# Issuing a decoder layer's transposed units from ScalarE's queue instead of SP's

## The chip, the core and the metric

The kernel runs on one core of a Trainium2 chip. The core has five engines that run side by side, each with its own instruction queue: TensorE (PE in the profile), VectorE (DVE), ScalarE (ACT), GpSimd (POOL) and SyncE (SP). SP computes nothing; it issues DMA transfers. ScalarE and GpSimd can issue transfers too, in between their own work. An instruction that waits holds back those behind it on its engine. The metric is the device time of one execution in microseconds (us).

## What is computed

One hybrid decoder layer on a sequence of 512 tokens of width 2048: a normalisation, one input projection whose columns feed three groups of heads, one output projection, a residual sum and a last normalisation.

```python
h = rmsnorm(x, norm_g)
proj = h @ w_in                      # 2048 x 8224, split into 19 parts
# A: 8 heads: compressed blocks, selected blocks, sliding window 512, mixed by gates
q_a = heads(a_q, A_HEADS)
o_a = gate[..., 0:1] * o_cmp + gate[..., 1:2] * o_slc + gate[..., 2:3] * o_win
y_a = o_a.reshape(bsz, T, A_WIDTH) * jax.nn.silu(a_z)
# B: mLSTM, 4 heads of 256, causal convolution before it, norm and two gates behind it
y_b = h_b.reshape(bsz, T, B_WIDTH) * jax.nn.silu(b_z)
# C: 8 heads, sliding window 128, with sinks
y_c = o_c.reshape(bsz, T, C_WIDTH) * jax.nn.silu(c_z)
mix = jnp.concatenate([y_a, y_b, y_c], axis=-1)
return x + mix @ w_out               # then rmsnorm with final_norm_g
```

## The kernel before

**The weight stream.** The two projections run through the whole kernel and set its order. The weights come in column groups (`groups`, then `outs`), each group in pieces of two (for `ck` four) row blocks of 128. A piece is loaded by SP (`dma_piece`, L140, 512 KB), split into a high and a low half by ScalarE (`wh`, L164 and L162) and VectorE (`wl`, L172 and L170), and multiplied on TensorE in three products for each row block (`mms`, L1149). While piece `pos` is multiplied, piece `pos + 2` is split and piece `pos + 5` is loaded at its end; there are three `raw` tiles.

**Steps and lanes.** A piece is multiplied in four parts, and behind each part, which is six matmuls, `step()` runs. It takes one turn of each generator in `lanes`: the heads' work is written as such generators, and `yield` ends a turn. So everything else is woven into the weight stream by hand, a step at a time, and the number of `yield`s between two pieces of work is the time that the first one has. The instructions then run in this order on each engine.

**The transposed units.** The softmax weights of A and C have queries on the partitions, and the product with the values needs keys there. `flip` turns them: for each part VectorE transposes blocks of 32 by 32 into `sq` (L613), the block is written to DRAM (`far`, L615) and read back in another order (`ptT` for A, `cptT` for C, L621). `a_out` flips eight units, one for each pair of heads and each of two branches, in six parts (widths 512, 512 and 256 for each of two heads); `c_out` flips four, in four parts (384 and 512 for each head). Behind the flip, `pause(PT_)` or `pause(PTC)` lets some steps pass, and then TensorE multiplies (`oT`, L952, and `coT`, L1035). Before the change SP issues all these transfers, in program order between the loads of weights.

**The same for B.** `hb_post` flips B's heads out in eight parts of 512 (tile `hb`), long before they are needed; `ev_bz` reads four of them back at once (`hbT`) behind the first part of groups `bz0` and `bz1`.

**What feeds the units.** `a_scores` works one unit ahead: scores on TensorE, a masked minimum on VectorE (L905), exponentials on ScalarE (L907), and scalings of the parts on ScalarE (L919) once VectorE has the sums' reciprocals (`wgt`, L913 and L914). It starts a unit only when the one before the last has been multiplied (`done`). `c_scores` does the same for C (L995, L998, L1004, L1012).

Of the kernel before, what the change touches and what calls it, by code (L numbers as in the profile page):

```python
# [27 lines left out]
T, D, P = 512, 2048, 128  # L28
# [32 lines left out]
def hymba_layer(ctx, tc, x, norm_g, w_in, w_out, pe_k, w1_k, w2_k, pe_v, w1_v, w2_v, conv_w, conv_b,  # L61
                i_bias, f_bias, mnorm_g, sinks, final_g, consts, out):
    nc = tc.nc
    PE, ACT, DVE, POOL, SP = nc.tensor, nc.scalar, nc.vector, nc.gpsimd, nc.sync
# [9 lines left out]
    def U(name, dt=F32):  # L74
        return ar.tile([P, 516], dt, tag="u", name=name)
# [3 lines left out]
    def WK(name):  # L79
        return ps.tile([P, 512], F32, tag="wk", bufs=4, name=name)  # L80
# [223 lines left out]
    p = WK("gT")  # L304
# [303 lines left out]
    def flip_out(src, tag, bufs):  # L608


        n = src.shape[1]
        sq, far = U("sq"), dr.tile([P * 512], F32, name="far", tag=tag, bufs=bufs)
        DVE.transpose(sq[:, :n].rearrange("p (j b t) -> p b j t", j=4, t=32),  # L613
                      src.rearrange("p (b k j) -> p b j k", j=4, k=32))
        SP.dma_start(far[:P * n].rearrange("(p f) -> p f", p=P), sq[:, :n])  # L615
        return far, n

    def flip_in(far, name):

        dst, (src, n) = U(name), far  # L620
        SP.dma_start(dst[:, :n].rearrange("p (q f) -> p q f", q=4),  # L621
                     src[:P * n].rearrange("(q p f) -> p q f", q=4, p=P))
        return dst[:, :n].rearrange("p (q b t) -> p b q t", q=4, t=32)

    def hb_post(pair, ssq):
        yield from pause(3)
        for t in range(4):
            hb, th = B["hb", pair, t], U("bsq")
            for q in range(2):
                ACT.activation(th[:, q * 256:(q + 1) * 256], hb[:, q * 256:(q + 1) * 256], AF.Square,  # L630
                               accum_out=ssq[:, 2 * t + q:2 * t + q + 1])
            yield
        r = S("br", 8, 2)
        rsqrt(r, ssq, 256, "b")
        DVE.tensor_scalar(r, r, 0.5, None, op0=OP.mult)
        yield
        for t in range(4):
            hb = B["hb", pair, t]
            for q in range(2):
                s = slice(q * 256, (q + 1) * 256)  # L640
                DVE.tensor_scalar(hb[:, s], hb[:, s], r[:, 2 * t + q:2 * t + q + 1], None, op0=OP.mult)
            yield

        B["hbT", pair] = []
        for t in range(4):
            B["hbT", pair].append(flip_out(B.pop(("hb", pair, t))[:, :512], "hbT", 8))
            yield
# [3 lines left out]
    def ev_bz(pair):  # L651
        def ev(c, acc):
            z = U("zf")
            scaled(z[:, :512], acc)
            if c == 0:
                B["hbT", pair] = [flip_in(x, "hbT") for x in B["hbT", pair]]
            start(bz_post(pair, c, z))
        return ev
# [198 lines left out]


    PB = {0: (1, 384), 1: (2, 0), 2: (1, 0), 3: (0, 0)}
    PT_, PTC = 6, 8  # L860
    ready = {}

    def flip(parts, name):

        far, back = [], []
        for i in range(len(parts)):
            far.append(flip_out(parts[i], "far", 8))
            parts[i] = None
            if i >= 2:
                back.append(flip_in(far[i - 2], name))  # L870
            yield
        return back + [flip_in(x, name) for x in far[-2:]]

    def a_scores():
        while B["cmp"] in lanes:
# [48 lines left out]
    def a_out():  # L924
        n = 0
        for pr in range(4):
# [3 lines left out]
            for br, vo in ((1, 0), (2, 128)):  # L930
                while n not in ready:
                    yield
                pt = ready.pop(n)
                yield from pause(PA)
                bl = ((3, 3, 3, 3), (2, 2, 2, 0), (1, 1))
                parts = [pt[h].pop(0)[:, :P * len(b)] for h in hs for b in bl]
                del pt
                back = yield from flip(parts, "ptT")
                tt = {h: {(j, b % (j + 1)): back[3 * q + u][:, b] for u in range(3) for b, j in enumerate(bl[u])}
                      for q, h in enumerate(hs)}  # L940
                yield from pause(PT_)

                if br == 1:
                    ob = WK("oT")
                    for q in range(2):
                        o = (pr % 2) * 128 + 64 * q
                        PE.matmul(ob[64 * q:64 * q + 64], vbd[g][:, o:o + 64], PCT[g][:, :512],
                                  start=True, stop=False, skip_group_check=True)
                for i in range(4):
                    for j in range(i, 4):  # L950
                        for q, h in enumerate(hs):
                            PE.matmul(ob[64 * q:64 * q + 64, j * P:(j + 1) * P], VG[i][:, vo + 64 * g:vo + 64 * g + 64],  # L952
                                      tt[h][j, i], start=False, stop=(br == 2 and i == 3), skip_group_check=True)
                done[n] = True
                n += 1
                yield
# [59 lines left out]
    def c_out():  # L1016

        blocks = [(0, 0), (1, 0), (1, 1), (2, 1), (2, 2), (3, 2), (3, 3)]
        for pr in range(4):
            while pr not in cready:  # L1020
                yield
            hs = (2 * pr, 2 * pr + 1)
            g = pr // 2
            pt = cready.pop(pr)
            yield from pause(PC)
            parts = [pt[h].pop(0)[:, 128 - 128 * u:512] for h in hs for u in range(2)]
            del pt
            back = yield from flip(parts, "cptT")
            tt = {h: {ji: back[2 * q + u][:, b] for u in range(2) for b, ji in enumerate(blocks[3 * u:3 + 4 * u])}
                  for q, h in enumerate(hs)}  # L1030
            yield from pause(PTC)
            ob = WK("coT")
            for n, (j, i) in enumerate(blocks):
                for q, h in enumerate(hs):
                    PE.matmul(ob[64 * q:64 * q + 64, j * P:(j + 1) * P], VG[i][:, 280 + 64 * g:344 + 64 * g],  # L1035
                              tt[h][j, i], start=(i < j or j == 0), stop=(i == j),
                              skip_group_check=True)
            cdone[pr] = True
            yield
            y_out("c", pr, ob)  # L1040
# [116 lines left out]
    for pos, (g, i) in enumerate(pieces):  # L1157
        np_ = KT // g.kps
        nct = g.n // P if g.mode == "F" else NT
        if i == 0:  # L1160
# [10 lines left out]
            if g.mode == "O":  # L1171
                n = int(g.name[3])
# [65 lines left out]
```

## Time and profile before

| | |
|---|---|
| three timed runs | 1027.75, 1028.22 and 1030.64 us, median 1028.22 |
| profiled execution, its own time | 1031.22 us |
| span from first to last instruction | 1029.5 us |
| granted TensorE clock, mean over the span | 0.989 of full speed |
| busy: PE, DVE, ACT, POOL | 1007.5, 585.6, 477.5, 21.5 us |
| writes `far<-sq` (L615) | 72, at 532.3 to 855.6 us |
| reads of `ptT`, `cptT`, `hbT` (L621) | 48, 16 and 8, at 536.8 to 860.9 us |

The profile is of one execution. A row with SPq or ACTq is a transfer's issue on that engine's queue; the transfer itself lands later. The page names a wait by what released it. The granted clock is what the chip allowed TensorE: 1.00 is 2.4 GHz, and the lower of its two levels is 1.2 GHz.

### The profile page before, as it was taken

The numbers are of one execution on the slowest core, as the hardware profiler recorded it, in microseconds if no ns is written. First come the engines' busy times: TensorE is split into PE (matmuls) and PEld (weight loads), VectorE is DVE, ScalarE is ACT, GpSimd is POOL, SyncE is SP. The second block draws the span as 40 slices with busy tenths as digits, with TensorE's granted clock in tenths as the row PEclk, the third lists the DMA queues.
The fourth block names the chain that finished last, engine by engine and source line by source line (L and its number), as shares of the span: only waits on it lengthen the run. The fifth ranks groups of instructions, "written<-read, shape, count | busy, mean of one in ns | idle before, by whom it ended". The sixth has DMA issues, their size and how long they took to land.

```text
span 1029.5 us, 13708 instructions
## 1 busy us (share of the span) xinstructions
PE 1007.5 (98%) x4967; PEld 835.0 (81%) x4967; DVE 585.6 (57%) x1253; ACT 477.5 (46%) x991; POOL 21.5 (2%) x40
## 2 busy tenths in 40 slices
PE   9999999999999999999999999999899899999996
PEld 7988888888888888888888788878777788888885
DVE  4563266664284847435566577856676575424434
ACT  6753244443253536234467474755654542323324
POOL 2400000000000000000000000000000000000000
PEclk9999999999999999999999999999999899999998
DMA  8633323232313244232335556555564685433214
GB/s 238 173 109 100 103 65 103 62 103 82 103 61 103 62 127 100 82 111 74 103 105 175 175 172 193 148 160 163 164 200 133 241 276 173 127 100 100 85 61 164
DMA packets 121092, 133.22 MB, mean 129 GB/s; under 512 B 23557, under 2 KB 81261, under 8 KB 120897
## 3 DMA queue, kind: packets, MB, share of 16 engines
q1 hardware_dynamic: 117792, 125.66, 40.9%
q0 software_dynamic: 2240, 6.23, 1.8%
q8 instruction: 39, 0.64, 0.3%
q10 hardware_dynamic: 992, 0.46, 0.2%
q14 instruction: 29, 0.23, 0.1%
HBM read 111.88 MB, written 20.45 MB: 129 GB/s over the span
## 4 chain that ended last, share of the span: by engine, by line
PE 86%; DVE 6%; DMA 5%; issue 1%; ACT 1%; SPq 0%; ACTq 0%; DVEq 0%
PE acc L1149 72%; DMA far<-sq 3%; DVE sq L613 2%; PE oT L952 2%; PE sp L561 1%; DMA ptT<-far 1%; PE acc L316 1%; PE acc L315 1%; PE acc L314 1%; DVE wl L172 1%; PE coT L1035 1%; PE sc L902 1%; PE sc L901 1%; PE xT L285 1%; DVE pp L905 0%
## 5 line engine op out<-in xcount | busy, mean ns | idle before, releaser
L1149 PE MATMUL acc<-hTh,wh 128*128 128x512 f32 x720 | 283.6, 394 | 0.0
L1149 PE MATMUL acc<-hTh,wl 128*128 128x512 f32 x720 | 281.5, 391 | 0.0
L1149 PE MATMUL acc<-hTl,wh 128*128 128x512 f32 x720 | 281.2, 391 | 0.0
L172 DVE SCALAR_TENSOR_TENSOR wl<-raw,gcol,wh 128x512 fp32r<-128x512 f32 (+1 forms) x256 | 179.0, 718 | 125.1 <-ACT wh L164 124.7
L164 ACT ACTIVATE wh<-raw,gcol 128x512 fp32r<-128x512 f32 (+1 forms) x256 | 171.2, 695 | 150.9 <-PE acc L1149 124.2
L1149 PEld LDWEIGHTS acc<-hTh,wl 128*128 128x128 f32 x720 | 135.4, 188 | 28.8
L1149 PEld LDWEIGHTS acc<-hTh,wh 128*128 128x128 f32 x720 | 135.6, 188 | 27.7 <-issue 1.7
L1149 PEld LDWEIGHTS acc<-hTl,wh 128*128 128x128 f32 x720 | 135.7, 188 | 25.8
L1149 PE MATMUL acc<-wh,hTh 128*128 128x512 f32 x256 | 101.2, 395 | 0.0
L1149 PE MATMUL acc<-wh,hTl 128*128 128x512 f32 x256 | 100.1, 391 | 0.0
L1149 PE MATMUL acc<-wl,hTh 128*128 128x512 f32 x256 | 99.9, 390 | 0.0
L1149 PE MATMUL acc<-wh,mixh 128*128 128x512 f32 x224 | 88.6, 396 | 0.0
L1149 PE MATMUL acc<-wh,mixl 128*128 128x512 f32 x224 | 88.1, 393 | 0.0
L1149 PE MATMUL acc<-wl,mixh 128*128 128x512 f32 x224 | 88.0, 393 | 0.0
L170 DVE TENSOR_TENSOR wl<-raw,wh 128x512 fp32r<-128x512 f32 x56 | 38.4, 689 | 55.7 <-ACT wh L162 55.4
L162 ACT CAST wh<-raw 128x512 fp32r<-128x512 f32 x56 | 34.0, 617 | 76.3 <-PE acc L1149 64.0
L1149 PEld LDWEIGHTS acc<-wh,hTl 128*128 128x128 f32 x256 | 48.0, 188 | 10.5
L1149 PEld LDWEIGHTS acc<-wh,hTh 128*128 128x128 f32 x256 | 48.1, 188 | 9.4 <-issue 0.4
L1149 PEld LDWEIGHTS acc<-wl,hTh 128*128 128x128 f32 x256 | 48.1, 188 | 9.0
L907 ACT ACTIVATE pp<-pp,nmx 128x512 f32<-128x512 f32 (+3 forms) x64 | 35.8, 559 | 35.1 <-DVE nmx L905 35.0
L905 DVE CUSTOM_DVE_ANT_0 pp<-sc,dmast 128x512 f32<-128x512 f32 (+3 forms) x64 | 31.1, 485 | 35.2 <-PE sc L902 35.0
L1149 PEld LDWEIGHTS acc<-wh,mixl 128*128 128x128 f32 x224 | 42.1, 188 | 10.0
(285 smaller groups left out, 1255.0 us busy)
## 6 DMA issues: line engine op xcount, KB each, us to landing
raw<-in_w_in_dram SPq DMA_DIRECT2D x80, 512.0 KB, 3.8
raw<-in_w_in_dram SPq DMA_DIRECT2D x68, 256.0 KB, 2.9
raw<-in_w_out_dram SPq DMA_DIRECT2D x32, 512.0 KB, 3.9
far<-sq SPq DMA_DIRECT2D x48, 256.0 KB, 2.8
ptT<-far SPq DMA_DIRECT2D x32, 256.0 KB, 3.9
xr<-in_x_dram POOLq DMA_DIRECT2D x4, 1024.0 KB, 8.3
x<-in_x_dram SPq DMA_DIRECT2D x12, 256.0 KB, 5.3
raw<-in_w_in_dram SPq DMA_DIRECT2D x8, 384.0 KB, 3.2
```

The lines of the kernel that those rows point to most:

```text
L162: ACT.copy(t["h"][:, q], raw[:, j + q])
L164: ACT.activation(t["h"][:, q], raw[:, j + q], AF.Copy, scale=gcol[:, k:k + 1])
L170: DVE.tensor_tensor(t["l"][:, q], raw[:, j + q], f(t["h"][:, q]), op=OP.subtract)
L172: DVE.scalar_tensor_tensor(t["l"][:, q], raw[:, j + q], gcol[:, k:k + 1], f(t["h"][:, q]), op0=OP.mult, op1=OP.subtract)
L285: PE.transpose(p[:, q * P:(q + 1) * P], X[t][c][:, q * P:(q + 1) * P], ident)
L314: PE.matmul(acc[:, :416], HH(k, *s), G0H[k][:, :416], start=(k == 0), stop=False)
L315: PE.matmul(acc[:, :416], HL(k, *s), G0H[k][:, :416], start=False, stop=False)
L613: DVE.transpose(sq[:, :n].rearrange("p (j b t) -> p b j t", j=4, t=32), src.rearrange("p (b k j) -> p b j k", j=4, k=32))
L905: DVE.tensor_tensor_reduce(b, sp[:, :nk], dmast[:, 512 - nk:], scale=-(2.0 ** -(h + 1)), scalar=3.0e38, op0=OP.add, op1=OP.min, accum_out= ...
L907: later(lambda b=b, h=h, j=j, st=st: ACT.activation(b, b, AF.Exp, scale=-1.0, bias=st[h][0][:, j:j + 1], accum_out=st[h][1][:, j:j + 1]))
L952: PE.matmul(ob[64 * q:64 * q + 64, j * P:(j + 1) * P], VG[i][:, vo + 64 * g:vo + 64 * g + 64], tt[h][j, i], start=False, stop=(br == 2 and ...
L1149: PE.matmul(accs[c][:, :n], a, b, start=(k == 0 and q == 0), stop=(k == KT - 1 and q == 2))
```

## The change

The writes of L615 and the reads of L621 are issued by ScalarE. In `flip`, the last two reads no longer stand together behind the last step: each takes a step of its own, so that every read stands two steps behind its write. The pauses behind the flip are one step shorter.

```diff
@@ flip_out @@
-        SP.dma_start(far[:P * n].rearrange("(p f) -> p f", p=P), sq[:, :n])
+        ACT.dma_start(far[:P * n].rearrange("(p f) -> p f", p=P), sq[:, :n])
         return far, n
@@ flip_in @@
         dst, (src, n) = U(name), far
-        SP.dma_start(dst[:, :n].rearrange("p (q f) -> p q f", q=4),
+        ACT.dma_start(dst[:, :n].rearrange("p (q f) -> p q f", q=4),
                      src[:P * n].rearrange("(q p f) -> p q f", q=4, p=P))
@@
-    PT_, PTC = 6, 8
+    PT_, PTC = 5, 7
@@ flip @@
             yield
-        return back + [flip_in(x, name) for x in far[-2:]]
+        for x in far[-2:]:
+            back.append(flip_in(x, name))
+            yield
+        return back
```

Counted in the program's order, in steps of six matmuls of L1149, the products of A's eight units stand at steps 331, 348, 365, 382, 403, 420, 437 and 454 before, and at 332, 350, 368, 388, 408, 426, 444 and 462 now; those of C's four at 455, 472, 489 and 506, and now at 456, 474, 492 and 510. Line numbers from L869 on are three higher in the changed kernel.

**ScalarE at A's second unit.** This is what ScalarE had between two splits of weights there: exponentials (`pp` with `sum`) and scalings (`pp` with `wgt`) of the unit that follows.

```order
L907 ACTIVATE pp_4967,sum_4971<-pp_4967,nmx_4970 128x256
L907 ACTIVATE pp_4963,sum_4969<-pp_4963,nmx_4968 128x128
L907 ACTIVATE pp_4966,sum_4971<-pp_4966,nmx_4970 128x128
L164 ACTIVATE wh_5124<-raw_4980,gcol_80 128x512
L164 ACTIVATE wh_5139<-raw_4980,gcol_80 128x512
L919 ACTIVATE pp_4962<-pp_4962,wgt_5149 128x512
```

And now:

```order
L615 DMA far_5110<-sq_5109 128x512
L621 DMA ptT_5113<-far_5077 128x4x128
L164 ACTIVATE wh_5117<-raw_4966,gcol_80 128x512
L910 ACTIVATE pp_4981,sum_4986<-pp_4981,nmx_4985 128x128
L615 DMA far_5128<-sq_5127 128x512
L621 DMA ptT_5131<-far_5093 128x4x64
L164 ACTIVATE wh_5133<-raw_4966,gcol_80 128x512
L615 DMA far_5144<-sq_5143 128x256
L621 DMA ptT_5147<-far_5110 128x4x128
L922 ACTIVATE pp_4977<-pp_4977,wgt_5156 128x512
```

A write waits for its step's transpose, a read for the landing of the write two steps before it; both now stand between the splits and the exponentials.

**A's last unit.** Before, SP had its transfers woven with those of C's first unit (`cptT`), and the weight load among them:

```order
L140 DMA raw_7002<-in_w_in_dram 128x2x512
L615 DMA far_7014<-sq_7013 128x512
L621 DMA ptT_7017<-far_6979 128x4x128
L615 DMA far_7023<-sq_7022 128x384
L621 DMA cptT_7026<-far_6983 128x4x96
L615 DMA far_7039<-sq_7038 128x512
L621 DMA ptT_7042<-far_6993 128x4x64
L615 DMA far_7051<-sq_7050 128x512
L621 DMA cptT_7054<-far_6999 128x4x128
L615 DMA far_7064<-sq_7063 128x256
L621 DMA ptT_7067<-far_7014 128x4x128
L621 DMA cptT_7072<-far_7023 128x4x96
```

Now ScalarE has, behind C's first unit:

```order
L621 DMA ptT_7108<-far_7082 128x4x128
L164 ACTIVATE wh_7112<-raw_6988,gcol_80 128x512
L621 DMA hbT_7123<-far_4963 128x4x128
L621 DMA hbT_7125<-far_4992 128x4x128
L621 DMA hbT_7127<-far_5011 128x4x128
L621 DMA hbT_7129<-far_5027 128x4x128
L615 DMA far_7132<-sq_7131 128x512
L621 DMA ptT_7135<-far_7093 128x4x64
L662 ACTIVATE zth_7137<-zf_7121 128x512
L164 ACTIVATE wh_7139<-raw_6988,gcol_80 128x512
L615 DMA far_7152<-sq_7151 128x256
L621 DMA ptT_7155<-far_7105 128x4x128
```

The two units no longer share steps, and the four reads of `hbT`, which stood behind the whole flip on SP, stand in the middle of it.

## Rows read from the trace of the kernel before

**Rows 1.** The page's busy times: engine, busy us, share of the span, instructions.
```profile
PE 1007.5 (98%) x4967; PEld 835.0 (81%) x4967; DVE 585.6 (57%) x1253; ACT 477.5 (46%) x991; POOL 21.5 (2%) x40
```

**Rows 2.** What PE waited for: us in total, times, longest us.
```profile
PE oT L952 <- DMA ptT<-far: 8.7, 5, 3.8
PE coT L1035 <- DMA cptT<-far: 2.7, 2, 1.6
```

**Rows 3.** PE's rows after an idle time: start, us, instructions, in brackets idle before.
```profile
579.55 0.44 PE L952 MATMUL oT<-ptT,vg 128*64 128x128 f32 x4 [1.68 <-DMA ptT<-far]
677.25 2.65 PE L952 MATMUL oT<-ptT,vg 128*64 128x128 f32 x38 [0.36 <-DMA ptT<-far]
740.41 4.17 PE L952 MATMUL oT<-ptT,vg 128*64 128x128 f32 x38 [2.59 <-DMA ptT<-far]
774.07 3.89 PE L952 MATMUL oT<-ptT,vg 128*64 128x128 f32 x38 [3.82 <-DMA ptT<-far]
807.92 0.40 PE L1035 MATMUL coT<-cptT,vg 128*64 128x128 f32 x2 [1.13 <-DMA cptT<-far]
809.90 3.42 PE L1035 MATMUL coT<-cptT,vg 128*64 128x128 f32 x26 [1.58 <-DMA cptT<-far]
```

**Rows 4.** The chain that ended last, whole span: start us, us, what.
```profile
572.80 5.14 DMA far<-sq
584.06 1.58 PE acc L1149 x6
586.10 1.39 PE acc L1149 x6
641.71 2.33 PE oT L952 x40
730.79 5.96 DMA far<-sq
797.81 7.20 DMA far<-sq
839.91 1.68 PE coT L1035 x28
```

**Rows 5.** Stretches: busy time of each engine, PE's granted clock, DMA share, GB/s.
```profile
775.00:780.00 5.00, 5.00 (x40) 4.12 (x38) 0.21 (x1) 0.00 (x0) 0.00 (x0) 0.66 1.08 342
810.00:815.00 5.00, 5.00 (x30) 4.08 (x31) 0.00 (x0) 1.33 (x2) 0.00 (x0) 0.50 1.01 342
705.00:745.00 40.00, 37.41 (x225) 30.59 (x224) 27.85 (x69) 25.90 (x65) 0.00 (x0) 0.96 0.48 144
```

**Rows 6.** SP's queue: start, us, instruction.
```profile
572.12 0.63 SPq L140 DMA_DIRECT2D raw<-in_w_in_dram  x1
729.83 0.56 SPq L140 DMA_DIRECT2D raw<-in_w_in_dram  x1
772.39 4.30 SPq L621 DMA_DIRECT2D hbT<-far  x4
```

**Rows 7.** VectorE's transposes in the same two stretches.
```profile
567.49 2.61 DVE L613 STREAM_TRANSPOSE sq<-pp 128x512 f32<-128x512 f32 x3
727.78 2.09 DVE L613 STREAM_TRANSPOSE sq<-pp 128x512 f32<-128x512 f32 x2
```

**Rows 8.** Line L615: issue time ns min/median/max; landing of its transfers, us.
```profile
L615 SPq DMA_DIRECT2D far<-sq x72: 319/333/1021, 532.3 to 855.6; - x72
DMA to landing us min/median/max: 1.7/2.7/7.2
```

**Rows 9.** The page's DMA issues: KB each, median us from issue to landing.
```profile
ptT<-far SPq DMA_DIRECT2D x32, 256.0 KB, 3.9
```

**Rows 10.** ScalarE at the start of the span.
```profile
4.70 0.39 ACTq L254 DMA_DIRECT2D raw<-in_w_in_dram  x1
5.40 0.20 ACT L294 ACTIVATE warm<-epst 128x1 f32<-128x1 f32 x1
```

**Rows 11.** What SP's queue waited for, those of L621.
```profile
SPq L621 <- DMA far<-sq: 30.0, 19, 3.7
```

## The prediction, made before the changed kernel was run

> **What bounds the kernel now.** I read the page's busy times first. TensorE is busy 98% of the span and every other engine at most 57% [rows 1], so the change can only pay, or cost, where TensorE stands still or runs slowly. TensorE's own waits come next: beside the start of the span it waits for one thing, the reads back from DRAM of the transposed units, 8.7 us for A's and 2.7 us for C's [rows 2]. I number A's eight units (pair and branch) A1 to A8 and C's four C1 to C4. TensorE's timeline places the idle time: it stands before the value products of A2, A5, A7, A8 and C2 and of no other unit [rows 3].
>
> Each of these stops costs more than its idle time. After the idle time at 770.25 us the granted clock of the next stretch is 0.66, after the one at 806.79 it is 0.50, with 1.00 the upper of the two levels (2.4 GHz) and 0.5 the lower (1.2 GHz) [rows 5]. So I take the whole cost of a stop: from the end of the work before it to the end of the unit's products, less what the same products take undisturbed, 2.33 us for an A unit and 1.68 us for a C unit [rows 4]. A2: 577.87 to 584.06 is 6.19, less 2.33 is 3.86. A5: 676.89 to 679.90, so 0.68. A7: 737.82 to 744.58, so 4.43. A8: 770.25 to 777.96, so 5.38. C2: 806.79 to 813.32, less 1.68, so 4.85 [rows 3, 4]. Together 19.2 us, of which 11.4 are idle [rows 2] and 7.8 slow clock. That is all there is to win. (A2's own idle time is what the others leave of A's 8.7: 1.9 us.)
>
> **The change, term by term.** *One step more.* A step is six accumulating matmuls, 1.39 us [rows 4]. Every unit's products now stand eight steps behind its last write instead of seven. If all landings stayed where they are, the idle times would shrink by 1.39 each: A2 1.9 to 0.5, A5 0.36 to nothing, A7 2.59 to 1.20, A8 3.82 to 2.43, C2 2.71 to 1.32.
>
> *SP's queue.* SP issued writes and reads in one order with the weight loads. In A2 the last transpose ends at 570.10 [rows 7], its write starts at 572.80 [rows 4], since SP stood at an earlier read and a weight load [rows 6]. On ScalarE no weight load stands ahead of it, so up to 2.70 us come back, more than A2's 0.5. In A7 the transpose of the fifth part ends by 729.87 [rows 7] and its write starts at 730.79, behind the weight load of 729.83 [rows 4, 6]: 0.92 back, which leaves 0.28.
>
> *Landing.* The writes that held A2, A7 and C2 landed after 5.14, 5.96 and 7.20 us [rows 4]; the median is 2.7 [rows 8]. The first two have a 512 KB weight load issued on the same queue 0.7 and 1.0 us before them [rows 6]. No row shows a write on a queue apart from the loads, so I bound it: nothing gained, or landing at the median, which is 2.4, 3.3 and 4.5 us. I take about half for C2, which leaves it under 1 us of idle time and, with the clock, 1.5 us of its 4.85; the rest of A7 vanishes.
>
> The Trainium skill speaks against this term: "DMA: Bandwidth & Descriptors", section "Issuing engines are not separate DMA queues", says that transfers issued from several engines run on the same 16 engines and that only the issuing time is saved. By that, the landing term is nothing and the saving is about 9 us. The same page, "Queues, rings and completion order", has SP and ScalarE own a ring each, served in turn packet by packet; by that, a write need not wait for a whole load ahead of it and about 14 us are saved. The row that would decide does not exist before the change.
>
> *A8.* Before, A8 and C1 are flipped in the same steps, twelve transfers woven into each other on SP. Each A unit is now at least one step longer, so A8's products move from step 454 to 462 while C1's move from 455 to 456. That separates them and takes away what made A8 late. In exchange the four hbT reads now stand in the middle of A8's flip on ScalarE. They took 4.30 us to issue on SP [rows 6], and A8's fifth and sixth writes come behind them. From sixth write to products there are 8 x 1.39 = 11.1 us; a write of 2.7 to 5.1 us [rows 4, 8] and a read of 3.9 [rows 9] need 6.6 to 9.0. That leaves 2.1 to 4.5 us against the 4.3. I take a short stop, 1.5 us with its clock, in place of 5.38.
>
> *ScalarE pays.* It issues 72 writes and 72 reads more. At 0.333 us for a write [rows 8], and about the same for a read, that is some 50 us of issuing. This is hidden so far as the engine has work queued: at the start a DMA was issued at 4.70 while an ACTIVATE that stands ahead of it in the program ran only at 5.40 [rows 10]. Its busiest flip stretch has 25.9 us of 40 busy [rows 5], so the time itself fits. The waits matter more. Each write waits for VectorE's transpose of its own step, each read for a landing, and behind them on ScalarE stand the weight halves wh, the exponentials and the scalings. VectorE's wl waits for wh, and TensorE for both. SP waited 30.0 us for landings in 19 reads, 3.7 at most [rows 11]. Bounds: nothing, or 30 us if all of it passed to TensorE. A weight half is made in the piece two ahead of its use, some six steps or 8.3 us before it, and one hold is less than half of that; also, reads now stand two steps behind their writes throughout. So I take the low end, 2.5 us in all.
>
> *Weight loads* leave SP sooner; nothing waits for them on TensorE, so that is worth nothing. PE, VectorE and POOL have the same instructions as before, and no arithmetic changes.
>
> **Sum.** Kept of 19.2: A2 3.9, A5 0.7, A7 4.4, A8 3.9, C2 3.3, together 16.2; less 2.5 is 13.7. The profiled execution took 1031.2 us against a median of 1028.2; I subtract from the median: 1014.5 us.
>
> **Rivals.** *Landings do not improve* (chance 0.20). The bytes are the same and the DMA engines are full in these stretches, share 1.08 and 1.01 [rows 5]; so each write lands as late as now. Then C2 keeps 1.3 us of idle time plus about 1.9 of clock, A8 2.4 plus 1.6, A7 0.3: 7.5 of 19.2 stay, and with ScalarE's 2.5 the gain is 9.2: 1019 us. For it: full engines. Against: the median write lands in 2.7 us [rows 8]. The first rule of the Trainium skill above would end here.
>
> *ScalarE is as late as SP was* (0.13). The last two reads stand behind scalings that wait for VectorE, and behind landings; then writes and reads start as late as before, the stops move with the step, and what the step gives (5.9 us of idle time) goes into held weight halves: 1025 to 1031 us. For it: around A7 ScalarE is busy 25.9 of 40 us before any of this [rows 5]. Against: DMAs are issued past queued work [rows 10].
>
> *ScalarE becomes the bound* (0.20), slower. The place is A7, A8 and the second hbT block; the mechanism is a hold at a landing or at the 4.3 us of hbT reads, on top of VectorE's own lag, which makes wh late, wl later, and TensorE stop inside the accumulations. It decides once ScalarE lags by more than six steps, 8.3 us. Two holds of 3.7 and an hbT block in one flip reach that. At 4 us of idle and 1.9 of clock in four units it costs 24, less 12 still saved: 1040 us.
>
> **Numbers.** Forecast 0.47, the three rivals 0.20, 0.13 and 0.20. Within 0.3% (3.1 us) counts as no change, about what this measurement can tell. Faster: 0.67, same 0.13, slower 0.20. The floor is all stops gone, 1009 us; nothing in the rows reaches below it, and that is the low end. The forecast and the first two rivals end at 1031; some of the third lies just above, so 1034 is the high end and leaves out most of that rival. The forecast alone spans 1009 to 1018.
>
> **What would show it.** Right: TensorE's waits for ptT and cptT under 3 us; the clock at 1.00 through 570 to 800 us; writes on ScalarE's queue that start within half a microsecond of their transpose, with a median landing still near 2.7 but no 6 or 7 us behind weight loads; A8 and C1 products some 10 us apart. Wrong: TensorE idle before L1149 with a release by wl or wh; VectorE waiting for wh by tens of microseconds more than now inside the flips; reads that start late after their write has landed; hbT reads at 0.8 us and more each on ScalarE with A8 stopped behind them.

## The result, and the profile after

The changed kernel takes 1016.02 us in the median of 4 runs (1015.69 to 1017.95), the kernel before in the same comparison 1027.99 us (1027.65 to 1030.64): ratio 0.9882, 95% interval [0.9861, 0.9903]. That is 12.0 us saved, where 13.7 were forecast.

The profiled execution of the change, first the page's busy times (columns as in [rows 1]):

```profile
PE 999.4 (99%) x4967; PEld 826.7 (82%) x4967; DVE 587.9 (58%) x1253; ACT 477.0 (47%) x991; POOL 21.5 (2%) x40
```

TensorE is busy 8.1 us less than in [rows 1], for the same 4967 matmuls: that is mainly the slow clock of before (the mean granted clock is 0.997 where it was 0.989). Its own waits (us in total, times, longest us), those at the start of the span left out:

```profile
PE acc L1152 <- DVE zf L373: 1.4, 1, 1.4
...
PE csc L992 <- DVE nmx L998: 0.8, 1, 0.8
PE acc L1152 <- ACT wh L164: 0.6, 1, 0.6
PE acc L1152 <- DVE wl L170: 0.6, 2, 0.3
PE csc L992 <- DVE nmx L908: 0.4, 1, 0.4
PE acc L1152 <- ACT wh L162: 0.2, 1, 0.2
```

The 11.4 us for `ptT` and `cptT` of [rows 2] are gone to the last one. In their place stand 4.0 us of waits that the kernel before did not have, all on work that comes from VectorE and ScalarE. The account closes: 11.4 idle + 8.1 busy - 4.0 new waits is 15.5, and the spans differ by 15.6 (1029.5 to 1013.9). The profiled execution of before was 3.2 us above its median and that of the change 0.3 below, so the medians differ by 12.0.

TensorE's timeline at the products of A2, A7, C1, A8 and C2 (start, us, instructions, idle time before in brackets where there is any):

```profile
580.14 2.50 PE L955 MATMUL oT<-ptT,vg 128*64 128x128 f32 x40
...
744.18 2.35 PE L955 MATMUL oT<-ptT,vg 128*64 128x128 f32 x40
...
763.02 1.75 PE L1038 MATMUL coT<-cptT,vg 128*64 128x128 f32 x28
...
776.11 2.40 PE L955 MATMUL oT<-ptT,vg 128*64 128x128 f32 x40
...
796.26 1.75 PE L1038 MATMUL coT<-cptT,vg 128*64 128x128 f32 x28
```

No brackets, and each unit in one piece of its undisturbed length ([rows 3, 4] for before). C1 now comes 13.1 us ahead of A8. The granted clock is the last figure but two of a stretch (columns as in [rows 5]):

```profile
770.00:780.00 10.00, 9.21 (x74) 7.70 (x74) 9.96 (x31) 8.68 (x26) 0.00 (x0) 1.00 0.46 140
820.00:830.00 10.00, 8.58 (x57) 6.57 (x56) 3.10 (x6) 3.41 (x6) 0.83 (x2) 1.00 1.05 365
```

```profile
823.45 0.50 PE L1152 MATMUL acc<-wh,mixh 128*128 128x512 f32 x1 [1.42 <-DVE zf L373]
```

It stays at 1.00, though TensorE stands still for 1.42 us in the second stretch.

### The profile page after: what moved, and what is told of

It is laid out like the page before. It is cut to its first block, busy times and chain, and to the rows that moved or that the text cites. A ratio compares the mean times of both kernels' runs of the same rounds, so it can differ in the third digit from the quotient of the medians.

```text
span 1013.9 us, 13633 instructions
## 1 busy us (share of the span) xinstructions
PE 999.4 (99%) x4967; PEld 826.7 (82%) x4967; DVE 587.9 (58%) x1253; ACT 477.0 (47%) x991; POOL 21.5 (2%) x40
## 4 chain that ended last, share of the span: by engine, by line
PE 84%; DVE 6%; DMA 5%; ACT 2%; issue 1%; ACTq 1%; DVEq 0%
PE acc L1152 72%; DMA far<-sq 2%; DMA hbT<-far 2%; PE sp L561 1%; DVE sq L613 1%; PE acc L316 1%; PE acc L315 1%; PE acc L314 1%; PE oT L955 1%; DVE wl L172 1%; PE sc L905 1%; PE sc L904 1%; ACTq L621 1%; PE xT L285 1%; DVE zf L667 1%
## 5 line engine op out<-in xcount | busy, mean ns | idle before, releaser
L1152 PE MATMUL acc<-hTh,wh 128*128 128x512 f32 x720 | 283.2, 393 | 0.6 <-ACT wh L164 0.6
L1152 PE MATMUL acc<-hTh,wl 128*128 128x512 f32 x720 | 281.1, 390 | 0.1
L1152 PE MATMUL acc<-hTl,wh 128*128 128x512 f32 x720 | 280.7, 390 | 0.0
L1152 PEld LDWEIGHTS acc<-hTh,wl 128*128 128x128 f32 x720 | 135.1, 188 | 29.6 <-DVE wl L172 0.5
L1152 PEld LDWEIGHTS acc<-hTh,wh 128*128 128x128 f32 x720 | 135.2, 188 | 28.3 <-ACT wh L164 1.2
L1152 PEld LDWEIGHTS acc<-hTl,wh 128*128 128x128 f32 x720 | 135.3, 188 | 25.6
L1152 PE MATMUL acc<-wh,hTh 128*128 128x512 f32 x256 | 101.2, 395 | 0.0
L1152 PE MATMUL acc<-wh,hTl 128*128 128x512 f32 x256 | 100.1, 391 | 0.0
L1152 PE MATMUL acc<-wl,hTh 128*128 128x512 f32 x256 | 99.9, 390 | 0.0
L1152 PE MATMUL acc<-wh,mixh 128*128 128x512 f32 x224 | 88.7, 396 | 1.6 <-DVE zf L373 1.4
L1152 PE MATMUL acc<-wl,mixh 128*128 128x512 f32 x224 | 88.4, 395 | 0.6 <-DVE wl L170 0.6
L1152 PE MATMUL acc<-wh,mixl 128*128 128x512 f32 x224 | 88.3, 394 | 0.0
L1152 PEld LDWEIGHTS acc<-wh,hTl 128*128 128x128 f32 x256 | 48.0, 188 | 10.4
L1152 PEld LDWEIGHTS acc<-wh,hTh 128*128 128x128 f32 x256 | 48.1, 188 | 9.4 <-issue 0.3
L1152 PEld LDWEIGHTS acc<-wl,hTh 128*128 128x128 f32 x256 | 48.1, 188 | 9.0
L1152 PEld LDWEIGHTS acc<-wh,mixh 128*128 128x128 f32 x224 | 42.1, 188 | 12.3 <-DVE zf L373 1.8
L1152 PEld LDWEIGHTS acc<-wl,mixh 128*128 128x128 f32 x224 | 42.1, 188 | 11.5 <-DVE wl L170 2.0
```

The lines of the kernel that those rows point to most:

```text
L1152: PE.matmul(accs[c][:, :n], a, b, start=(k == 0 and q == 0), stop=(k == KT - 1 and q == 2))
```

## The experiments

All times are medians, all ratios are to runs of the kernel before on the same chip; e1 to e8 ran on one chip, e9 to e12 on another. "Reads" is TensorE's waits for `ptT` and `cptT` in the profiled execution, "other" its remaining waits except those at the start, both in us.

| run | queue | what stands otherwise than before | us | ratio [95%] | reads | other |
|---|---|---|---|---|---|---|
| before | SP | | 1027.99 | | 11.4 | 0 |
| the change | ScalarE | pause behind +1, reads apart | 1016.02 | 0.9882 [0.9861, 0.9903] | 0 | 4.0 |
| e1 | SP | pause behind +1, reads apart | 1017.63 | 0.9891 [0.9862, 0.9921] | 3.5 | 0.7 |
| e2 | ScalarE | nothing | 1034.83 | 1.0062 [1.0041, 1.0083] | 14.9 | 2.0 |
| e3 | ScalarE | as the change, hbT reads on SP | 1018.24 | 0.9901 [0.9875, 0.9926] | 0 | 6.7 |
| e4 | SP | nothing | 1026.89 | 0.9990 [0.9969, 1.0010] | 10.8 | 0 |
| e5 | ScalarE | as the change | 1017.94 | 0.9882 [0.9861, 0.9902] | 0 | 7.0 |
| e6 | SP | pause ahead +1 | 1012.64 | 0.9843 [0.9825, 0.9861] | 1.5 | 0 |
| e7 | SP | pause behind +1 | 1015.17 | 0.9870 [0.9849, 0.9890] | 1.1 | 0.5 |
| e8 | SP | reads apart | 1032.19 | 1.0032 [1.0017, 1.0047] | 13.0 | 0 |
| e9 | ScalarE | pause ahead +1 | 1029.78 | 1.0026 [1.0012, 1.0039] | 5.1 | 8.3 |
| e10 | SP | A7 and A8 seven steps later | 1015.14 | 0.9882 [0.9864, 0.9899] | 2.6 | 0 |
| e11 | SP | C's low q off VectorE | 1027.10 | 0.9995 [0.9982, 1.0009] | 9.8 | 0 |
| e12 | SP | pause ahead +2 | 1022.41 | 0.9952 [0.9937, 0.9968] | 8.3 | 1.6 |

The theory at the outset was the prediction's: the step gives part, the queue the rest. Its rivals: the queue does nothing, or it does all.

**e1, the step without the queue.**

```diff
 # the changed kernel, with L615 and L621 as before:
-        ACT.dma_start(...)
+        SP.dma_start(...)
```

> Writes and reads stay on SP's queue; only the last two reads stand a step apart and the pauses are one shorter, so every unit's products stand where the change puts them. My theory: the step and the separation of A8 from C1 give part of the gain, the queue the rest. TensorE's waits for ptT and cptT stay at 3 to 5 us, mainly at C2 and A7, and the time is 1017 to 1021 us. Rival, the queue does nothing: the waits are gone here too, and the time is that of the whole change (1016) or, without ScalarE's new waits (4 us), 1012 to 1014. Rival, the queue does all: within 3 us of the kernel before.

1017.63 us, the time of the change within what can be told. Waits of TensorE:

```profile
PE coT L1038 <- DMA cptT<-far: 2.2, 1, 2.2
PE oT L955 <- DMA ptT<-far: 1.3, 2, 0.7
```

Short stops are left, at C4 and A2, not at the two units that my theory named. Time and waits (3.5 us) lie in my ranges, but the step alone brings all of the gain, as the first rival has it. Against the change on the same chip (e5, 1017.94) the queue takes 3.5 us of waits for reads away and puts 4.0 to 7.0 us of others in their place.

**e2, the queue without the step.**

```diff
 # the kernel before, with L615 and L621 as in the change:
-        SP.dma_start(...)
+        ACT.dma_start(...)
```

> Writes and reads on ScalarE's queue, the steps as before the change (last two reads together, longer pauses, products one step earlier, A8 and C1 flipped in the same steps). My theory: A2, A7 and A5 lose their stops, for their writes start earlier; A8 and C2 keep stops of 1 to 4 us with their slow clock; ScalarE costs 2 to 4 us: 1017 to 1022 us. Rival, the queue does nothing: waits for ptT and cptT as before, 10 to 12 us, plus ScalarE's cost: 1028 to 1032. Rival, the queue does all: 1014 to 1017 us, no wait for ptT or cptT.

1034.83 us: slower than before, beyond all three expectations. Waits of TensorE:

```profile
PE oT L952 <- DMA ptT<-far: 12.6, 5, 4.2
PE coT L1035 <- DMA cptT<-far: 2.3, 3, 1.7
```

A2, A5, A7, A8 and C2 all stop again, A5 for 2.7 us instead of 0.36. My theory falls here: on its own the queue saves nothing and costs 6 us. Why is seen at A5's flip, on ScalarE and then on VectorE:

```profile
667.67 0.34 ACTq L615 DMA_DIRECT2D far<-sq  x1
668.05 1.25 ACT L723 CAST k2h<-kvf 64x512 fp32r<-64x512 f32 x2 [2.03 <-DVE sq L613]
669.33 1.34 ACT L164 ACTIVATE wh<-raw,gcol 128x512 fp32r<-128x512 f32 x2
```

```profile
670.09 0.75 DVE L172 SCALAR_TENSOR_TENSOR wl<-raw,gcol,wh 128x512 fp32r<-128x512 f32 x1 [1.81 <-ACT wh L164]
...
670.97 0.62 DVE L613 STREAM_TRANSPOSE sq<-pp 128x256 f32<-128x256 f32 x1
```

ScalarE stood 2.03 us until VectorE's transpose let the write go; the weight half behind the write came late, VectorE waited 1.81 us for it, and the next transpose, for which ScalarE's next write waits, stands behind that. So the two engines hold each other. Between 530 and 870 us VectorE waits 56.6 us for weight halves, 28.8 before the change.

**e3, hbT's reads back on SP.**

```diff
-                B["hbT", pair] = [flip_in(x, "hbT") for x in B["hbT", pair]]
+                B["hbT", pair] = [flip_in(x, "hbT", SP) for x in B["hbT", pair]]
```

> The changed kernel, with the eight reads of hbT alone back on SP's queue. My theory: what the change lost again (4.0 us of new waits on TensorE) hangs in part on these reads, which stand on ScalarE ahead of A8's last two writes and C3's tail: the waits of 0.79 us at 771 us and 1.42 us at 823 us go, the others stay, 1 to 3 us faster than the change (1013 to 1015). Rival, VectorE's lag or the weights cause them: the same time as the change within 1 us. Rival, hbT lands later on SP behind weight loads: TensorE's wait behind zf grows, 1017 to 1020.

1018.24 us, no difference from the change. One of the two waits that my theory named is gone, the one behind `zf` at 823 us (1.42 us in the change, 1.16 in e5 below). The other is not, 1.40 us before the scores at 772.69 (1.39 in e5), and small waits for weight halves from 835 us on bring the sum to 6.7 us, as against 7.0 in e5. So the hbT reads cause one of these waits at most, and the time does not depend on them.

**e4, the kernel before, and e5, the change, once more.** Neither has an edit.

> The kernel before once more, unchanged. The profiled execution of before took 1031.2 us, 3 us more than its median. If the stops at the reads differ between executions, this profile has other idle times in front of the value products, 6 to 11 us in sum, with a span that follows them; if the 3 us lie elsewhere, the waits are again 11.4 us at a time near 1028.

> The changed kernel once more, unchanged, on the same chip as its parts. If ScalarE's queue is worth nothing beside the step, it takes within 3 us of the run with the step alone (1017.6), and of the run with the pauses alone below. If the queue adds to the step, it is 3 to 6 us faster than those.

e4's profiled execution took 1029.1 us with 10.8 us of waits for reads and TensorE busy 1005.1 us, against 1031.2, 11.4 and 1007.5 [rows 1, 2]: the stops with their clock differ by 3 us between two executions of one program, and the spans by 2.2. e5 is the change again: the same ratio, no wait for reads, 7.0 us of other waits in this profile against 4.0 in the first.

**e6, the shift alone.** The pause ahead of each flip grows, the one behind it stays.

```diff
-PA, PC, ... = 4, 4, ...
+PA, PC, ... = 5, 5, ...
```

> The kernel before, all on SP's queue, with the pause ahead of every flip one step longer and nothing else: the products of all twelve units stand at the very steps of the change, but still only seven steps behind their last write. Theory of the separation: A7 and A8 lose their stops, since they no longer meet VectorE's work on q and C1's flip; A2, A5, C2 and C4 keep theirs, by the rows of the run with the step alone 2.6, 0.4, 0.9 and 3.6 us of idle time, 7.5 in all: 1020 to 1025 us. Theory of the slack: what counts is the distance from write to products, which is as before, so the waits are 10 to 12 us and the time 1026 to 1030.

1012.64 us, the lowest median of all, and faster than the change on the same chip (1017.94), though the intervals of the two ratios touch at 0.9861. Both theories fell short of it. Waits of TensorE:

```profile
PE coT L1035 <- DMA cptT<-far: 0.8, 1, 0.8
PE oT L952 <- DMA ptT<-far: 0.7, 2, 0.4
```

With not one step more between write and products, 1.5 us of 11.4 are left, at A1 and C2, whose last writes took 6.5 and 6.8 us to land. SP's rows around the last write of A7 and of A8 (start, us, instruction), and the products that follow:

```profile
735.94 0.51 SPq L615 DMA_DIRECT2D far<-sq  x1
...
766.25 0.64 SPq L615 DMA_DIRECT2D far<-sq  x1
```

```profile
745.06 2.35 PE L952 MATMUL oT<-ptT,vg 128*64 128x128 f32 x40
...
775.92 2.40 PE L952 MATMUL oT<-ptT,vg 128*64 128x128 f32 x40
```

A7 has 9.1 us from its last write to its products, A8 9.7. The same distance, from the traces, for the units that stopped (in us; "late" is by how much the last write started after its own step, which is found by counting 42 accumulating matmuls back from the products, 48 in the change):

| unit | before | late | e6 | late | the change | late |
|---|---|---|---|---|---|---|
| A2 | 4.6 | 5.0 | 8.6 | 1.0 | 6.8 | 4.2 |
| A5 | 5.3 | 5.3 | 6.9 | 3.6 | 7.7 | 4.2 |
| A7 | 5.7 | 6.1 | 9.1 | 3.4 | 12.4 | 1.4 |
| A8 | 3.6 | 6.0 | 9.7 | 3.8 | 10.9 | 5.0 |
| C2 | 5.3 | 4.4 | 7.6 | 2.0 | 8.3 | 3.9 |

Seven steps are 9.7 us. Before, the five units that stopped are the five whose last write started 4.4 us and more behind its step; of the other seven none was over 3.1. In e6 none of the five is. For A7 and A8 there is room beside that: scores and C1's products now fall between the step of the write and the products, 12.5 and 13.5 us of TensorE's work where 11.7 and 9.6 stood. In the change the distance grew otherwise. Only A7's last write came much nearer its step (4.7 us); those of A2, A5, A8 and C2 came 0.5 to 1.1 us nearer, and the extra step gave each 1.4 us. A8 has 15.9 us of TensorE's work between step and products there.

How much of this stood with VectorE and how much with SP before the change, the traces show. VectorE's last transposes of A5 and A7, and SP's writes of them:

```profile
670.59 0.63 DVE L613 STREAM_TRANSPOSE sq<-pp 128x256 f32<-128x256 f32 x1
...
731.09 0.64 DVE L613 STREAM_TRANSPOSE sq<-pp 128x256 f32<-128x256 f32 x1
```

```profile
671.24 0.33 SPq L615 DMA_DIRECT2D far<-sq  x1
...
731.75 0.57 SPq L615 DMA_DIRECT2D far<-sq  x1
```

SP issued each write 0.03 us behind its transpose. Of the 26.7 us by which the five last writes were late, 22.4 had passed when VectorE ended the transposes; SP added 2.7 us at A2, 1.5 at A8 and 0.03 at each of the others. What held VectorE (it waits for ScalarE's weight halves as well) is not in these rows.

**e7, the pause behind alone, and e8, the reads apart alone.**

```diff
 # e7: the kernel before with
-    PT_, PTC = 6, 8
+    PT_, PTC = 7, 9
 # e8: the change's flip on SP with
-    PT_, PTC = 5, 7
+    PT_, PTC = 4, 6
```

> The kernel before, all on SP's queue, both last reads still together, with the pause behind every flip one step longer and nothing else. If the reads' own steps are worth nothing, it is the run with the step alone: waits for ptT and cptT of 3 to 4 us, 1015 to 1020 us. If a read that SP holds too early delays the next, the waits are 2 us and more above that run and the time is 1020 to 1024.

> All on SP's queue, the last two reads a step apart each, the pauses two steps shorter than before, so that every unit's products stand at the steps of before. Separation and slack are both as before: waits of 10 to 13 us, 1026 to 1031 us. Rival, the reads' own steps carry the gain: waits under 5 us, 1016 to 1020.

e7: 1015.17 us, reads 1.1; its interval overlaps that of e6. So the units may be moved by a pause on either side of the flip. e8, with every unit at its old step: 1032.19 us, 13.0 us of waits for reads. Separate reads on SP do not help; by e8's interval they cost 1.7 to 4.8 us, which is also about what e1 lacks against e7.

**e9, the shift and the queue.** e6's edit and e2's together.

> The run with the shift alone (1012.6 us), with writes and reads moved to ScalarE's queue as in the change: the queue and nothing else. Theory of the mutual hold: ScalarE stands at a write until VectorE's transpose, the weight halves behind it are late, and VectorE's next halves wait for those; the waits for wl, wh, zf and the scores that the change has (4 to 7 us) come here too, or stops of 2 to 4 us at A2 or A5: 1015 to 1020 us. Rival, the queue is worth nothing either way: 1011 to 1014. Rival, the queue helps once the units are apart: under 1011, with no wait for ptT or cptT.

1029.78 us, 17 us above e6 (19 by the ratios, since e6 ran on the other chip), where the mutual hold was expected to cost 2 to 7. Waits of TensorE:

```profile
PE coT L1035 <- DMA cptT<-far: 3.0, 1, 3.0
PE oT L952 <- DMA ptT<-far: 2.1, 2, 1.7
PE csc L989 <- DVE nmx L995: 1.9, 1, 1.9
PE acc L1149 <- DVE zf L373: 1.8, 2, 1.1
PE acc L1149 <- DVE qf L373: 1.6, 1, 1.6
PE acc L1149 <- DVE wl L172: 1.4, 2, 0.9
...
PE acc L1149 <- DVE wl L170: 1.2, 4, 0.4
```

These waits (13.4 us, 1.5 in e6) and a TensorE that is busy 1002.9 us instead of 997.6 make up the 17. How a queue on ScalarE reaches TensorE is seen at A6. ScalarE, the last write, the last read and what stood behind it:

```profile
705.44 0.33 ACTq L615 DMA_DIRECT2D far<-sq  x1
...
709.98 0.37 ACTq L621 DMA_DIRECT2D ptT<-far  x1
...
710.39 0.72 ACT L164 ACTIVATE wh<-raw,gcol 128x512 fp32r<-128x512 f32 x1 [1.70 <-DMA far<-sq]
```

VectorE, and then TensorE:

```profile
711.15 0.75 DVE L172 SCALAR_TENSOR_TENSOR wl<-raw,gcol,wh 128x512 fp32r<-128x512 f32 x1 [4.86 <-ACT wh L164]
...
711.82 0.68 DVE L373 TENSOR_TENSOR qf<-acc,R 128x512 f32<-128x512 f32 x1
```

```profile
712.55 0.50 PE L1149 MATMUL acc<-hTh,wh 128*128 128x512 f32 x1 [1.56 <-DVE qf L373]
```

The read of 709.98 waited for the write of 705.44 to land. The weight half behind it started at 710.39 after ScalarE had stood still for 1.70 us, VectorE's `wl` had waited 4.86 us for it (ScalarE's scalings of the unit are in that, too), `qf`, which empties TensorE's accumulator, came late behind that, and TensorE waited 1.56 us for it.

**e10, A7 and A8 alone moved.**

```diff
-                yield from pause(PA)
+                yield from pause(PA + (7 if n == 6 else 0))
```

> The kernel before, all on SP's queue, with seven steps more ahead of A7's flip and nothing else: A7 and A8 move to steps 444 and 461, A1 to A6 and C1 to C4 stay where they were, and every unit keeps seven steps from write to products. Theory of the separation: the stops of A7 and A8 go (2.6 and 3.8 us of idle time, 9.8 with the slow clock), A2, A5 and C2 keep theirs (1.9, 0.4, 2.7): 1018 to 1021 us. Theory of the slack: A7 and A8 stop as before, 1026 to 1030.

1015.14 us. Waits of TensorE:

```profile
PE oT L952 <- DMA ptT<-far: 1.5, 3, 0.6
...
PE coT L1035 <- DMA cptT<-far: 1.1, 2, 0.7
```

A7 and A8 run through; A2, A5 and C2 still stop, 0.6, 0.5 and 1.1 us, and A1 for 0.3, less than expected in sum (A2's products came 0.9 us later in this execution, its flip did not; C2's last write landed after 4.4 us instead of 7.0). Moving the two units brings 12 of the 16 us that e6 saves. Their last writes are still late, 4.3 and 6.3 us behind their steps: the stops went because 12.5 and 13.5 us of TensorE's work now stand between step and products. A8's last write is as late in e1 and e7 (6.5 and 6.4 us), and there, too, A8 runs through.

**e11, C's low q off VectorE.**

```diff
-            DVE.scalar_tensor_tensor(t[b, :512], qf[a, :512], sc, ..., op1=OP.subtract)
+            if nm == "c":
+                ACT.activation(t[b, :512], qf[a, :512], AF.Copy, scale=sc)
+            else:
+                DVE.scalar_tensor_tensor(t[b, :512], qf[a, :512], sc, ..., op1=OP.subtract)
```

> The kernel before, all steps and queues as they were; the eight low halves of C's q (L700, 0.69 us each, 5.5 us) are no longer computed on VectorE: ScalarE copies the high half in their place, so C's scores lose their low part. Theory of VectorE's backlog: A7's last transposes stood behind them, its last write comes 3 to 5 us sooner after its step (6.0 us before), A7's stop of 2.6 us goes and with it its slow clock, A8 and the others stay: 1022 to 1026 us. If A7 stops for its landings or its queue, it stops by 2 us or more here too: 1026 to 1030.

1027.10 us, no difference. A7 still waits 1.6 us. VectorE at A7's flip:

```profile
721.66 0.75 DVE L172 SCALAR_TENSOR_TENSOR wl<-raw,gcol,wh 128x512 fp32r<-128x512 f32 x1 [2.90 <-ACT wh L164]
...
724.96 0.75 DVE L172 SCALAR_TENSOR_TENSOR wl<-raw,gcol,wh 128x512 fp32r<-128x512 f32 x1 [1.19 <-ACT wh L164]
```

It no longer computes the low halves but waits 2.90 and 1.19 us for weight halves, which on ScalarE stand behind the copies that took their place. The work was moved to the engine that VectorE waits for, so this run does not clear VectorE's backlog, and it does not show that the backlog is VectorE's alone. A7's last write started 4.9 us behind its step, 6.1 before, and the stop is 1.6 us against 2.6 before and 2.0 in e4: the direction expected, but too little to settle A7.

**e12, two steps.**

```diff
-PA, PC, ... = 4, 4, ...
+PA, PC, ... = 6, 6, ...
```

> The pause ahead of every flip two steps longer than before instead of one. Theory of the separation: the run with one step left 1.5 us of waits for ptT and cptT, so there is nothing more to win: 1010 to 1014 us. If the units meet other work again (A8 now stands at step 470, C2 at 476), stops come back at those units, 1015 to 1022. If the later products delay the end, waits for mixed tiles show behind 860 us and the time is above 1014.

1022.41 us. A8 (now at step 470) stops once for 5.5 us, C3 three times for 2.8 together:

```profile
PE oT L952 <- DMA ptT<-far: 5.5, 1, 5.5
PE coT L1035 <- DMA cptT<-far: 2.8, 3, 1.3
```

The time lies just above the range that was named for new stops. A8's last write starts at 784.70, 2.7 us ahead of its products and 0.03 us after VectorE has ended the transpose, 6.9 us behind its step; C3's last write took 10.9 us to land. More distance between units is not better in itself: what counts is where each flip falls.

## Why the prediction came out

The time was right, and most of the reasons were not. Most of the signs that were named came: no wait for reads, the clock at 1.00, no landing of 6 us and more, A8 and C1 13 us apart, and 69 of the 72 writes within half a microsecond of their transpose (the other three up to 2.8 us behind it). But e6 shows nearly the same on SP: they were signs that the stops are gone, not of why. Two signs of being wrong came in small, too: TensorE was idle for 1.4 us before L1152 (L1149 before the change) with a release by `wl` or `wh`, and VectorE waited 46.1 us for weight halves between 530 and 870 us, 28.8 before.

*What bounds the kernel* held. TensorE's stops with their slow clock were all that could be won, and all of the 19.2 us went: 11.4 idle and 8.1 of busy time. The bound itself was some 1.6 us too low. A2, A5, A7 and A8 had each multiplied two products before they stopped, 0.4 us that the sum leaves out of the stop but counts in the 2.33. At A8:

```profile
769.82 0.43 PE L952 MATMUL oT<-ptT,vg 128*64 128x128 f32 x2
```

*One step more* named only part of what a step does. The prediction said: "If all landings stayed where they are, the idle times would shrink by 1.39 each". They did not stay. The units moved by one step each, which adds up along the chain (A7 by 7 steps, A8 by 8, C4 by 4), so other work stood around each flip. In e6 that alone brought the writes 1.7 to 4.0 us nearer their step, put more of TensorE's work behind those of A7 and A8, and saved the most, with none of the 1.39; e8 has the change's separate reads at the old steps and saves nothing. In the change itself the 1.39 did come as slack at A2, A5 and C2, more than their writes gained on their steps; at A7 the displacement gave 4.7 us. The term left the displacement out for every unit but A8.

*SP's queue* failed. At A7 it was read from the fifth part; the last write, the sixth, stood only 0.03 us behind its transpose on SP. The 2.70 us of A2 came back with SP still issuing: in e6 A2's last transpose ends at 573.2 and its write starts at 573.27, while A7's last write stands 2.5 us behind its transpose on SP, more than before, and A7 does not stop. With ScalarE issuing and the steps as before (e2), A2's last write was held 1.1 us instead of 2.7, but its transpose ended 1.4 us later behind its step, and A2 stopped longer.

*Landing* failed too. Over all 72 writes, landing us min/median/max, of the change and of e1, which has the same steps on SP:

```profile
DMA to landing us min/median/max: 1.7/3.1/5.7
```

```profile
DMA to landing us min/median/max: 1.7/3.2/6.9
```

Before it was 2.7 in the median [rows 8]; neither is shorter. C2's last write did land sooner, after 5.1 us instead of 7.0, but on SP it took 6.8 in e6 and 3.6 in e1, so this does not go with the queue. This is where the Trainium skill was right against me: "DMA: Bandwidth & Descriptors", section "Issuing engines are not separate DMA queues", says that transfers started by several engines run interleaved on the same 16 DMA engines and only the time of issuing is saved. The traces agree as far as the landing goes, 3.2 us on SP against 3.1 on ScalarE. What the prediction drew from the same page's section "Queues, rings and completion order", that a write need not wait for a load ahead of it, is borne out by no run here: the longest landing is 5.7 us in the change, but 6.8 in e9, 6.9 in e2 and 7.3 in e3, also on ScalarE, and 7.2 before.

*A8* held in its main part. The new steps took A8 and C1 apart and A8's stop went, with SP (e1, e6, e10) as with ScalarE. The hbT reads did hold A8's last two writes, 2.8 and 1.8 us behind their transposes, and the last write started 5.0 us behind its step. The stop of 1.5 us that this was to leave did not show, because 15.9 us of TensorE's work, C1's products and C's scores in it, stand between that step and A8's products, where the prediction counted 11.1.

*ScalarE pays* had the right mechanism and too small a size: 2.5 us were taken, 4.0 and 7.0 us of new waits stand in the two profiles of the change, 6 us in e2's time and 17 in e9's. The chain that the prediction gave for its slow rival (hold, `wh` late, `wl` late, TensorE stops) is the one seen at A6 in e9. The prediction set its limit at a lag of six steps, 8.3 us; at A6 a hold of 1.70 us and a `wl` that waited 4.86 us were enough, since it was not the weight half itself but `qf` behind it that ran out of time. That the transposes wait behind `wl` and so come late themselves, as in e2, was not foreseen.

So the sum came near partly by luck. In the profiles all of the stops went, 19.5 us where 16.2 were to go, and 4.0 us of new waits took their share where 2.5 were allowed; and the stops had been read from an execution 3 us slower than the median from which the sum was taken. That the shift alone saves 16 us (e6) where step, queue, landing and A8 were to give 16.2 is coincidence, for two of those four terms gave nothing. By these runs the change is a shift that saves 11 to 16 us and a queue that adds nothing: e1 and e7 reach its time on SP.

*The rivals.* "Landings do not improve" had its premise right and its result wrong, since the stops went without shorter landings. The two on ScalarE did not come about in the change, but e2 and e9 are what they look like.

*What stays open.* Which of VectorE's work makes the last transposes late before the change: e11 did not name the culprit at A7, and at A2, A5 and C2 nothing was tried; nor was it shown by a run which of that work the shift takes out of the way in e6. And why ScalarE's queue costs 17 us in e9 but little in the change: between them lie one step of slack and the reads' own steps, and no run has one without the other on that queue.

**A version that beats both** is e6: the kernel before with two pauses a step longer, no queue moved, 1012.64 us, ratio 0.9843 [0.9825, 0.9861]. By its interval it can't be told from e7 (1015.17 us).

## What to carry to other kernels

Where units are chained, a pause of one step is not local slack alone: it moves every later unit, and its worth depends on what the other engines have queued where each flip then falls and on how much of the pacing engine's work then stands behind it. Read the distance from each unit's last write to its use, before and after, and split it: how late is the write behind its own step, and which engine made it late? Test a change of two parts by its parts, for here the part that looked like the point (the queue) cost time on its own and the incidental one gave it. A transfer issued from an engine that computes makes that engine wait for whatever the transfer waits for, and everything behind it too, as at A5 in e2 (2.03 us) and at A6 in e9 (1.70 us).

## What the runs showed of the hardware

Not every stop was followed by a lower clock. Behind the idle times at A8 (3.82 us) and C2 (1.13 and 1.58) the granted clock was 0.66 and 0.50 [rows 3, 5]; in the change the stretch with 1.42 us of idle time stayed at 1.00. What tells them apart no run was made to show. And the same program varies by more than the bound that I set: 26 runs of the kernel before lay between 1023.18 and 1031.68 us on one chip, so that 3 us can be told only from medians of several runs.
